# Hybrid gated block: the last block's projected tiles and first x tiles, and the list's price for the sums' loads

## The chip, the cores and the metric

The kernel runs on one core of one Trainium2 chip. The metric is the device time of one execution in microseconds. Before the change it is 2861.07 us, the median of three runs (2854.05 to 2863.21).

## What is computed

A layer of a streaming encoder, on x of 2048 tokens by 1024 features in float32. Only the end of the mixer and what follows it matters here:

```python
y = sigmoid(ga) * (att @ w_att_proj) + sigmoid(gm) * (mlstm_out @ w_mlstm_proj)
x = x + y @ w_out
hn = rms_norm(x, ffn_norm_g)
x = x + square(relu(hn @ w_up)) @ w_down
return rms_norm(x, final_norm_g)
```

`att` is a banded attention over chunks of 64, `mlstm_out` a recurrent matrix memory, and both read projections of the normed x.

## The kernel before

**Tiles and products.** The tokens are cut into four blocks of 512 (b = 0 to 3), the features into eight tiles of 128 (j = 0 to 7); a working tile is 128 x 512, 256 KB. Each float32 product is made of three fp32r products of 512 columns, from a high part (ScalarE, lines 427 and 971) and a rest (VectorE, lines 429, 976, 978) of each operand. Blocks are taken in pairs, 0 with 1 and 2 with 3, and the large products of a pair are done by a scheme with 7 instead of 8 sub-products (`quad`, line 571 in the trace). For it, sums of operand tiles and of weight tiles are needed. Per quad, seven operand sets A[0] to A[6] are used in order; A[0] and A[1] are the tiles k and 4 + k of the first block of the pair, and A[2] to A[6] need the second block as well. One quad is 7 x 24 = 168 products.

**Weights' sums.** `sum_w` makes the weights' sums of a quad once and keeps them in memory: per half, four loads of 256 KB into four `ctx` buffers (line 391), four subtractions on VectorE (line 396), four stores. They run beside other stages, from the second projection of block 0 to the first up quads, and stand last in rank.

**The last blocks.** After the down product of blocks 0 and 1, `project(2)` and `project(3)` multiply the mixers' outputs with their projections, tile pairs in the order 0, 2, 1, 3, which gives the tiles j in the order 0, 1, 4, 5, 2, 3, 6, 7. `load_gates` brings gate tiles into `temp` buffers (line 789), `merge` multiplies gate and bank (line 797), adds the two branches (line 805) and stores the result to `ypd[b]` (line 2101). `take_y_low` loads block 2's tiles for A[0] and A[1] (line 1731). Once `project(3)` is through, `take_y_rest(k)` for k = 0 to 3 takes five `ctx` buffers, loads two tiles of each block (line 1743), makes four sums (line 1749) and splits five operands. Then come the two output quads of blocks 2 and 3. `after_out` loads the x tiles to which they are added (`load`, line 2049, eight tiles one after another) and adds them (line 2062); the new x goes to memory and into the operands of the up quads that follow.

**Buffers.** There are 16 `ctx` buffers, 6 `temp` buffers, 28 operand buffers (`rpool`) and 8 PSUM banks. All users of `ctx` share the 16.

**Order.** The program is written out by a list planner (`Flow`): each step is a generator that yields the engine that it needs, its cost in ns and, for a load, the time to its landing, as in `yield "sp", 900, 2000`; steps carry a rank, and waits and buffers delay them. The planner's order is the program's order. From it the framework makes the queue of each engine, and it may pull an instruction ahead of earlier ones when its data and its buffers are free; the program's order is then the priority. On the chip each queue is worked through in order. All DMAs are issued from SyncE's queue.

Of the kernel before, what the change touches and what calls it, by code (L numbers as in the profile page):

```python
# [45 lines left out]
N_G, N_O, N_F = 2, 2, 8  # L46
# [47 lines left out]
class Flow:  # L94
# [8 lines left out]
               dve=dict(pe=220.0, act=130.0, dve=130.0, pool=155.0), pool=dict(pe=290.0, act=130.0, dve=60.0),  # L103
               sp=dict())
# [110 lines left out]
def dve_ns(n):  # L215
    return 70 + 1.042 * n
# [7 lines left out]
class Layer:  # L224
# [156 lines left out]
    def sum_w(self, q):  # L381

        fl, V = self.fl, self.nc.vector
        for h in range(2):
            got = yield "get", self.ctx, 4
            a, b, c, d = (x[:, :512] for x in got)
            wf, td = (t[:, :, h * 512:h * 512 + 512] for t in (self.io["wf"][q], self.td[q].ap()))
            kept = [Event() for _ in range(4)]
            for n, x in ((0, a), (1, c), (3, d), (2, b)):
                yield "sp", 900, 2000  # L390
                self.nc.sync.dma_start(x, wf[n])
            for n, dst, x, y in ((0, a, c, a), (2, c, d, c), (1, a, d, a), (3, b, b, a)):
                if n == 1:
                    yield "wait", [kept[0]]
                yield "dve", dve_ns(512)
                V.tensor_sub(dst, x, y)  # L396
                fl.spawn(self.store(td[n], dst, kept[n]), 1)
            yield "wait", kept
            fl.put(self.ctx, *got)
            fl.set(self.td_ev[q][h])  # L400
# [228 lines left out]
    def dense(self):  # L629
        fl = self.fl  # L630
# [51 lines left out]
        self.banks.want = 0  # L682
        O, X, U = self.operands(), self.operands(), self.operands()
        for i in range(N_G):
# [12 lines left out]
        for i, name in enumerate(IN_ORDER):  # L697
# [3 lines left out]
            if last:  # L701
                for k in range(4):
                    fl.spawn(self.take_x2(0, k, *U), 2)
            if i == 1:
# [4 lines left out]
                yield from self.quad(*X, self.after_in(name), release=last)  # L709
        for s in range(NS):  # L710
            if s == 1:
                U = self.operands()
                for i in range(N_O):
                    if i == N_O - 1:
                        for k in range(2):
                            fl.spawn(self.take_x2(1, k, *U), 2)
                    yield from self.quad(*O, self.after_out(1, i, U), release=i == N_O - 1)
            for i in range(N_F):
                if s == 0 and len(IN_ORDER) + i in EARLY_SUMS:
                    fl.spawn(self.sum_w(EARLY_SUMS[len(IN_ORDER) + i]), 3)  # L720
                if i == 2:
                    for h in range(2):
                        fl.spawn(self.norm_mid(s, h), 3)
                if i == N_F - 2:
                    D = {}, {(m, c): [Event() for _ in range(4)] for m in ORDER for c in range(4)}
                    ring = Pool([])
                    fl.spawn(self.take_u(s, ring, *D), 0)
                if s == 0 and i == N_F - 2:
                    fl.spawn(self.gates_far(2), 3)
                if s == 0 and i == N_F - 1:  # L730
                    for b in (2, 3):
                        fl.spawn(self.recurrence_far(b), 1)
                        fl.spawn(self.attention_far(b), 1)
                yield from self.quad(*U, self.after_up(s, i), release=i == N_F - 1)
            fl.spawn(self.final(s), 2 if s else -1)
            self.banks.want = 4
            for p, m in enumerate(ORDER):
                if p == 1:
                    fl.spawn(self.residual(s), 2)
                if s == 0 and p == len(ORDER) - 1:  # L740
                    O = self.operands()
                    for b in (2, 3):
                        fl.spawn(self.take_mix(b), 1)
                yield from self.down(s, m, ring, *D)
            self.banks.want = 0
            for b in (2, 3) if s == 0 else ():
                yield from self.project(b)
                for k in range(4):
                    fl.spawn((self.take_y_low if b == 2 else self.take_y_rest)(k, *O), 2)

    def take_mix(self, b):

# [4 lines left out]
            B["mix"][i] = r  # L757
            fl.spawn(self.take_u1(self.mixd[b].ap()[i], r, B["mix_ev"][i]), 1)

    def project(self, b):  # L760

        fl, B = self.fl, self.blk[b]
        gates = {}
        go = [Event() for _ in range(5)]
        fl.spawn(self.load_gates(b, gates, go), 1)
        for n, j in enumerate((0, 2, 1, 3)):
            att = {}
            fl.set(go[n + 1])
            for x in range(2):
                some = slice(4 * x, 4 * x + 4)  # L770
                bks = yield from self.pair_tile(B["mix"][some], B["mix_ev"][some], "get")
                for n in range(2):
                    fl.spawn(self.merge(b, x, 2 * j + n, bks[n], gates, att.setdefault(n, [None, Event()])), 1)
        fl.put(self.rpool, *B["mix"])
# [17 lines left out]
    def merge(self, b, x, j, bk, gates, att):  # L792
        fl, V = self.fl, self.nc.vector
        yield "wait", [gates[x, j][1]]
        g = gates[x, j][0]
        yield "dve", dve_ns(574)
        V.scalar_tensor_tensor(g[:, :512], g[:, :512], 1.0, bk, op0=ALU.add, op1=ALU.mult)
        fl.put(self.banks, bk)
        if x == 0:
            att[0] = g  # L800
            fl.set(att[1])
            return
        yield "wait", [att[1]]
        yield "dve", dve_ns(512)
        V.tensor_add(g[:, :512], g[:, :512], att[0][:, :512])
        fl.put(self.temp, att[0])
        fl.spawn(self.store(self.ypd[b].ap()[j], g[:, :512], self.yp_ev[b][j], self.temp, g), 1)
# [927 lines left out]
    def take_y_rest(self, k, A, aev):  # L1735

        fl, V = self.fl, self.nc.vector
        got = yield "get", self.ctx, 5
        a11, a12, a21, a22, s1 = (x[:, :512] for x in got)
        for b, j, a in ((2, k, a11), (2, 4 + k, a12), (3, k, a21), (3, 4 + k, a22)):  # L1740
            yield "wait", [self.yp_ev[b][j]]
            yield "sp", 900, 2000
            self.nc.sync.dma_start(a, self.ypd[b].ap()[j])
        done = []
        for m, dst, x, y in ((2, s1, a21, a22), (5, a21, a11, a21), (3, a11, s1, a11), (4, a12, a12, a11),
                             (6, a22, None, None)):
            if x is not None:
                yield "dve", dve_ns(512)
                (V.tensor_add if m == 2 else V.tensor_sub)(dst, x, y)
            fl.spawn(self.take_split(dst, m, k, A, aev, 0.5), 1)  # L1750
            done.append(aev[m][k])
        yield "wait", done
        fl.put(self.ctx, *got)
# [274 lines left out]
        fl.put(self.ctx, z)  # L2028
        fl.spawn(self.store(self.mfar[b].ap()[g], d5, self.m_ev[b, g], self.ctx, dst), 1)

    def after_out(self, s, q, U):

        fl, nc = self.fl, self.nc
        V = nc.vector
# [5 lines left out]
        hev = [{w: Event() for w in where} for _ in range(2)]  # L2040

        def load():
            for w in ("a11", "a22", "a12", "a21"):
                for n in range(2):
                    hi, h = where[w]
                    (x,) = yield "get", self.ctx, 1
                    xt[n][w] = x
                    yield "sp", 900, 2000
                    nc.sync.dma_start(x[:, :512], self.io["xt"][2 * s + h, 4 * hi + 2 * q + n])
                    fl.set(ev[n][w])  # L2050

        fl.spawn(load(), 1)
        for n in range(2 if s > 0 and q > 0 else 0):
            fl.spawn(self.spread(ht[n], hev[n], 2 * q + n, U), 1)
# [318 lines left out]
    def build(self):  # L2373
        fl, nc = self.fl, self.nc
# [15 lines left out]
        self.fin = [f32d(f"fin{h}", 4, P, T) for h in range(2)]  # L2390
        self.ud = f32d("u", 4, 7, 4, P, T)
        self.wi = 0
        self.wtile = {}
        self.wev, self.wgot = collections.defaultdict(Event), collections.defaultdict(Event)
        self.td_ev = {q: E(2) for q in (*range(N_G, N_G + N_O + N_USUM), *range(N_Q - N_F, N_Q + 2))}
# [111 lines left out]
```

## Time and profile before

| what | value |
|---|---|
| median of three runs | 2861.07 us (2854.05 to 2863.21) |
| the profiled execution | 2857.33 us |
| its span, first to last instruction | 2855.5 us |
| granted TensorE clock | 0.997 |
| VectorE busy | 2027.8 us (71%) |
| ScalarE busy | 1550.2 us (54%) |
| DMA read and written | 433.27 and 180.36 MB |

The page gives busy times of each engine and the chain of work that ended last. PE is TensorE, PEld its weight load, DVE is VectorE, ACT ScalarE, POOL GpSimd, SP SyncE; L571 is line 571 of the kernel. Times of rows in time are us from the start of the span. Since products overlap in the array, the busy time of PE is not the time that they need; the spacing of their starts is.

### The profile page before, as it was taken

To read this page: it belongs to the slowest core of one execution; us is meant where nothing else is said; L and a number is where in the kernel's file an instruction comes from. 1 tells how busy PE (TensorE), PEld (TensorE's weight loads), DVE (VectorE), ACT (ScalarE), POOL (GpSimd) and SP (SyncE) were. 2 spreads that over 40 slices of the span, in tenths; PEclk is the share of its full clock that TensorE was granted. 3 is DMA by queue.
4 is the path that set the end of the run, shared out by engine and by line. 5 is a ranking of instruction groups with operands and counts; after the bars stand their busy time and mean duration, and the time that the engine had idled before them with its cause. 6 is when DMAs were issued, how large, how long until landed. Compare 5 with 4: busy or idle time off the path is not lost.

```text
span 2855.5 us, 39050 instructions
## 1 busy us (share of the span) xinstructions
PE 2807.1 (98%) x13576; PEld 2342.3 (82%) x13576; DVE 2027.8 (71%) x3765; ACT 1550.2 (54%) x2679; POOL 47.8 (2%) x108
## 2 busy tenths in 40 slices
PE   8999999999999999999999999999999999999998
PEld 7888888888878888878888888887887788888887
DVE  6886479868896867876666788789668644455565
ACT  4664366755444545665555665566535655555444
POOL 0000000000000000000000000000000000000000
PEclk9999999999999999999999999999999999999999
DMA  6327732367765768587888967776697655566563
GB/s 218 99 90 256 243 113 88 126 194 248 253 220 191 240 225 290 172 274 273 299 277 285 280 213 234 209 241 222 218 309 245 202 199 195 197 236 213 188 223 134
DMA packets 283174, 616.24 MB, mean 216 GB/s; under 512 B 31712, under 2 KB 48224, under 8 KB 282976
## 3 DMA queue, kind: packets, MB, share of 16 engines
q1 hardware_dynamic: 282976, 613.75, 64.9%
q8 instruction: 106, 1.74, 0.2%
q14 instruction: 92, 0.75, 0.1%
HBM read 433.27 MB, written 180.36 MB: 215 GB/s over the span
## 4 chain that ended last, share of the span: by engine, by line
PE 82%; DVE 7%; DMA 5%; ACT 3%; issue 2%; POOL 0%; SPq 0%; POOLq 0%; DVEq 0%; ACTq 0%
PE bank L571 35%; PE bank L488 12%; PE bank L489 12%; PE bank L490 12%; PE bank L599 2%; PE bank L1228 2%; PE bank L1268 2%; DMA r<-u 2%; PE bank L1299 2%; DVE wsp L429 1%; DMA ctx<-in_wf 1%; DVE r L976 1%; DMA wsum<-ctx 1%; ACT wsp L427 1%; DMA sc<-x 0%
## 5 line engine op out<-in xcount | busy, mean ns | idle before, releaser
L571 PE MATMUL bank<-r,wsp 128*128 128x512 f32 x5208 | 1193.5, 390 | 15.1 <-DVE ctx L1819 8.4
L571 PEld LDWEIGHTS bank<-r,wsp 128*128 128x128 f32 x5208 | 977.2, 188 | 225.8 <-DVE ctx L1819 8.6
L429 DVE TENSOR_TENSOR wsp<-wraw,wsp 128x1024 fp32r<-128x1024 f32 x461 | 563.3, 1222 | 346.6 <-ACT wsp L427 330.5
L427 ACT CAST wsp<-wraw 128x1024 fp32r<-128x1024 f32 x461 | 484.1, 1050 | 493.3 <-PE bank L571 189.0
L488 PE MATMUL bank<-r,wsp 128*128 128x512 f32 x1600 | 640.5, 400 | 2.4 <-DVE r L1304 1.0
L490 PE MATMUL bank<-r,wsp 128*128 128x512 f32 x1600 | 624.9, 391 | 0.0
L489 PE MATMUL bank<-r,wsp 128*128 128x512 f32 x1600 | 624.7, 390 | 0.0
L490 PEld LDWEIGHTS bank<-r,wsp 128*128 128x128 f32 x1600 | 300.4, 188 | 64.8
L488 PEld LDWEIGHTS bank<-r,wsp 128*128 128x128 f32 x1600 | 301.1, 188 | 55.1 <-DVE r L1304 1.7
L489 PEld LDWEIGHTS bank<-r,wsp 128*128 128x128 f32 x1600 | 301.4, 188 | 51.2
L971 ACT CAST r<-r 128x512 fp32r<-128x512 f32 x240 | 146.2, 622 | 88.1 <-DMA r<-u 75.4
L976 DVE TENSOR_TENSOR r<-r 128x512 fp32r<-128x512 f32 x240 | 161.1, 688 | 41.6 <-ACT r L971 40.2
L1819 DVE TENSOR_TENSOR ctx<-bank,ctx 128x512 f32<-128x512 f32 x174 | 119.0, 687 | 82.5 <-PE bank L571 80.9
L1283 ACT ACTIVATE sc<-sc,scs 128x640 f32<-128x640 f32 (+4 forms) x128 | 97.4, 761 | 74.5 <-DVE scs L1280 71.9
L1811 ACT COPY ctx<-bank 128x512 f32<-128x512 f32 x174 | 100.9, 581 | 67.6 <-PE bank L571 62.1
L396 DVE TENSOR_TENSOR ctx<-ctx,ctx 128x512 f32<-128x512 f32 x112 | 76.7, 689 | 75.7 <-DMA ctx<-in_wf 60.2
L2178 ACT ACTIVATE ctx<-ctx 128x512 f32<-128x512 f32 x96 | 60.6, 632 | 110.5 <-DVE ctx L1819 110.4
L1274 DVE CUSTOM_DVE_ANT_0 sc<-bank,bias 128x320 f32<-128x320 f32 (+3 forms) x240 | 105.1, 461 | 16.7 <-PE bank L1268 13.9
L1228 PE MATMUL bank<-r,r 128*128 128x256 f32 (+1 forms) x672 | 107.8, 281 | 1.9 <-DVE r L1304 1.6
L1228 PEld LDWEIGHTS bank<-r,r 128*128 128x128 f32 x672 | 98.1, 189 | 12.8 <-DVE r L1304 4.6
L1304 DVE TENSOR_TENSOR r<-bank,r 128x512 fp32r<-128x512 f32 (+1 forms) x168 | 96.4, 594 | 6.5 <-ACT r L1302 5.5
L1268 PE MATMUL bank<-r,r 128*128 128x320 f32 (+3 forms) x480 | 88.1, 309 | 1.8 <-DVE ctx L1652 0.9
(290 smaller groups left out, 2837.7 us busy)
## 6 DMA issues: line engine op xcount, KB each, us to landing
wraw<-in_wf SPq DMA_DIRECT2D x170, 512.0 KB, 4.4
wraw<-wsum SPq DMA_DIRECT2D x136, 512.0 KB, 3.9
r<-u SPq DMA_DIRECT2D x224, 256.0 KB, 4.1
wraw<-in_w SPq DMA_DIRECT2D x104, 512.0 KB, 3.9
u<-ctx SPq DMA_DIRECT2D x128, 256.0 KB, 2.6
ctx<-in_wf SPq DMA_DIRECT2D x112, 256.0 KB, 4.4
wsum<-ctx SPq DMA_DIRECT2D x112, 256.0 KB, 3.9
u<-tmp SPq DMA_DIRECT2D x96, 256.0 KB, 3.3
```

Of the source, the lines that this page charges most:

```text
L427: nc.scalar.copy(w[:, 0], raw)
L429: nc.vector.tensor_sub(w[:, 1], raw, w[:, 0].bitcast(F32))
L488: mm(ps, lh, rh, start=first, stop=False)
L489: mm(ps, lh, rl, start=False, stop=False)
L490: mm(ps, ll, rh, start=False, stop=last)
L571: mm(ps, wv[:, x, k, n], a[:, y], start=new and k == 0 and x == y == 0, stop=k == 3 and x == 1, skip_group_check=True)
L971: self.nc.scalar.copy(dst[:, 0], src)
L976: self.nc.vector.tensor_sub(dst[:, 1], src, dst[:, 0].bitcast(F32))
L1228: nc.tensor.matmul(bk[:, c0:c0 + w], st, sl[:, x, o:o + w], start=n == 0, stop=n == total - 1)
L1268: nc.tensor.matmul(bks[x][:, :w], q[:, y, i * P:(i + 1) * P], kf[:, f * P + x * w:f * P + x * w + w], start=y == 0, stop=y == 1)
L1274: nc.vector.tensor_tensor_reduce(out=e[:, x * w:x * w + w], in0=bks[x][:, :w], in1=br[:, j0 + x * w:j0 + x * w + w], op0=ALU.add, op1=ALU. ...
L1819: nc.vector.tensor_add(t[:, o:o + 512], ps, t[:, o:o + 512])
```

## The change

Three things are edited. The result of `merge` for block 3 goes to a `ctx` buffer and stays there (`self.y3`), without store and load; `take_y_rest` uses these tiles as a21 and a22, and takes three `ctx` buffers of its own, one k at a time as the tiles appear. `take_y_rest` is spawned ahead of `project(3)`, with rank 1 instead of 2, and so is the first output quad's `after_out`, whose loads of x wait for an event that `project(3)` sets at its half. In the list, a load of `sum_w` takes 5000 ns to its landing, where it took 2000, and a load of `take_y_rest` 3000.

```diff
@@ sum_w
-                yield "sp", 900, 2000
+                yield "sp", 900, 5000
                 self.nc.sync.dma_start(x, wf[n])
@@ dense
             if s == 1:
-                U = self.operands()
...
-                    yield from self.quad(*O, self.after_out(1, i, U), release=i == N_O - 1)
+                    yield from self.quad(*O, self.after_out(1, i, U) if i > 0 else first_out, release=i == N_O - 1)
...
-            for b in (2, 3) if s == 0 else ():
-                yield from self.project(b)
+            if s == 0:
+                yield from self.project(2)
                 for k in range(4):
-                    fl.spawn((self.take_y_low if b == 2 else self.take_y_rest)(k, *O), 2)
+                    fl.spawn(self.take_y_low(k, *O), 2)
+                U = self.operands()
+                go = Event()
+                first_out = self.after_out(1, 0, U, go)
+                for k in range(4):
+                    fl.spawn(self.take_y_rest(k, *O), 1)
+                yield from self.project(3, go)
@@ project
+            if n == 2 and half is not None:
+                fl.set(half)
@@ merge
         yield "wait", [att[1]]
+        if b == 3:
+            (y,) = yield "get", self.ctx, 1
+            yield "dve", dve_ns(512)
+            V.tensor_add(y[:, :512], g[:, :512], att[0][:, :512])
+            fl.put(self.temp, att[0], g)
+            self.y3[j] = y
+            fl.set(self.yp_ev[3][j])
+            return
@@ take_y_rest
-        got = yield "get", self.ctx, 5
-        a11, a12, a21, a22, s1 = (x[:, :512] for x in got)
-        for b, j, a in ((2, k, a11), (2, 4 + k, a12), (3, k, a21), (3, 4 + k, a22)):
-            yield "wait", [self.yp_ev[b][j]]
-            yield "sp", 900, 2000
-            self.nc.sync.dma_start(a, self.ypd[b].ap()[j])
+        yield "wait", [self.yp_ev[3][k]]
+        got = yield "get", self.ctx, 3
+        a11, a12, s1 = (x[:, :512] for x in got)
+        for j, a in ((k, a11), (4 + k, a12)):
+            yield "sp", 900, 3000
+            self.nc.sync.dma_start(a, self.ypd[2].ap()[j])
+        yield "wait", [self.yp_ev[3][4 + k]]
+        got += [self.y3[k], self.y3[4 + k]]
+        a21, a22 = (x[:, :512] for x in got[3:])
@@ after_out, load
+            if go is not None:
+                yield "wait", [go]
```

More of the change, by code (lines that the diff above doesn't have):

```diff
@@ L758, in take_mix, with project @@
             fl.spawn(self.take_u1(self.mixd[b].ap()[i], r, B["mix_ev"][i]), 1)
-    def project(self, b):
+    def project(self, b, half=None):
         fl, B = self.fl, self.blk[b]
@@ L2029, in conv_far, with after_out @@
         fl.spawn(self.store(self.mfar[b].ap()[g], d5, self.m_ev[b, g], self.ctx, dst), 1)
-    def after_out(self, s, q, U):
+    def after_out(self, s, q, U, go=None):
         fl, nc = self.fl, self.nc
@@ L2392, in build @@
         self.wi = 0
+        self.y3 = {}
         self.wtile = {}
```

## The prediction

> **What bounds the kernel now.** I read the page first, then the chain of waits, then the busy time by stage.
>
> ```profile
> PE 2807.1 (98%) x13576; PEld 2342.3 (82%) x13576; DVE 2027.8 (71%) x3765; ACT 1550.2 (54%) x2679; POOL 47.8 (2%) x108
> ...
> PE 82%; DVE 7%; DMA 5%; ACT 3%; issue 2%; POOL 0%; SPq 0%; POOLq 0%; DVEq 0%; ACTq 0%
> ...
> 643.48 115.90 PE bank L571 x510
> ...
> 2358.51 169.49 PE bank L571 x747
> ```
>
> TensorE is busy 98% of the span, but its records overlap, so that says little. The two long unbroken stretches of the chain do: 169.49 / 747 = 0.227 us for each product of 512 columns, and 115.90 / 510 gives the same. I call this the full rate. A stage in which (number of products x 0.227) equals its length can't be shortened by anything on another engine; where it falls short, the difference is what the change can win. Windows over the stages that the change touches (columns: window, length, busy time and count of PE, PEld, DVE, ACT, POOL, granted clock, DMA share, GB/s):
>
> ```profile
> 990.00:1000.00 10.00, 8.54 (x39) 6.78 (x38) 7.82 (x9) 3.30 (x4) 0.00 (x0) 1.00 0.97 322
> 1105.00:1115.00 10.00, 8.70 (x39) 6.93 (x38) 7.39 (x10) 3.32 (x4) 0.00 (x0) 1.00 0.97 317
> 1260.00:1275.00 15.00, 11.09 (x48) 8.51 (x47) 8.04 (x11) 8.01 (x13) 0.00 (x0) 1.00 0.86 278
> 1300.00:1310.00 10.00, 8.46 (x38) 6.70 (x37) 6.02 (x8) 4.26 (x7) 0.00 (x0) 1.00 0.82 267
> ...
> 2086.00:2130.00 44.00, 44.00 (x195) 36.42 (x194) 29.73 (x39) 10.74 (x12) 0.00 (x0) 1.00 0.95 325
> 2130.00:2140.00 10.00, 10.00 (x46) 8.28 (x45) 8.57 (x14) 5.88 (x9) 0.00 (x0) 1.00 0.79 281
> 2140.00:2150.00 10.00, 6.67 (x26) 4.25 (x24) 8.86 (x14) 4.70 (x8) 0.00 (x0) 1.00 0.86 268
> 2150.00:2162.00 12.00, 8.63 (x25) 5.21 (x26) 11.66 (x20) 6.26 (x10) 0.00 (x0) 0.86 0.79 254
> 2162.00:2249.00 87.00, 86.93 (x384) 71.67 (x383) 71.40 (x101) 55.22 (x86) 0.00 (x0) 1.00 0.69 224
> 2249.00:2258.00 9.00, 7.14 (x25) 5.41 (x24) 5.13 (x7) 7.06 (x11) 0.00 (x0) 0.81 0.61 207
> 2258.00:2530.00 272.00, 272.00 (x1209) 225.45 (x1208) 132.75 (x164) 148.40 (x214) 0.00 (x0) 1.00 0.60 202
> ```
>
> The last block's projection (2086 to 2130, 195 products) runs at full rate: 195 x 0.227 = 44.3 of 44 us. So do 2162 to 2249 (87.2 of 87) and 2258 to 2530. The start of the output quads does not: from 2130 to 2162 stand 46 + 26 + 25 = 97 products, 22.0 us of work in 32 us, **10.0 us lost**. At 2249 to 2258, 25 products leave 3.3 us lost. In the four short windows of the weights' sums 1.1 + 1.1 + 4.1 + 1.4 = **7.8 us** are lost. So the change's three places hold 21.1 us together, 0.74% of the run.
>
> What TensorE waits for from 2130 to 2162, and what VectorE does there (its groups, then single rows in time):
>
> ```profile
> PE bank L571 <- DVE ctx L2062: 3.4, 2, 1.7
> PE bank L571 <- ACT r L973: 2.8, 4, 1.3
> ...
> L978 DVE SCALAR_TENSOR_TENSOR r<-ctx,r 128x512 fp32r<-128x512 f32 x19 | 12.9, 685 | 0.3 <-ACT r L973 0.2
> L1749 DVE TENSOR_TENSOR ctx<-ctx,ctx 128x512 f32<-128x512 f32 x16 | 10.8, 684 | 3.0 <-DMA ctx<-yp 3.0
> ...
> 2131.43 0.69 DVE L1749 TENSOR_TENSOR ctx<-ctx,ctx 128x512 f32<-128x512 f32 x1 [3.03 <-DMA ctx<-yp]
> ...
> 2149.90 0.69 DVE L2062 TENSOR_TENSOR ctx<-bank,ctx 128x512 f32<-128x512 f32 x1 [1.14 <-DMA ctx<-in_xt]
> ```
>
> The bound there is VectorE, busy 8.57 + 8.86 + 11.66 = 29.1 of 32 us: all 16 sums (L1749) and 19 of the 20 splits (L978) of the operands from `take_y_rest` fall into this stretch, and the first starts at 2131.43, after TensorE has left the projection. Its two idle times, 3.0 and 1.1 us, are the loads that the change removes or moves.
>
> **The change part by part.**
>
> *Straight into the operands.* Before, a tile of block 3 is added (L805), stored, and loaded again:
>
> ```profile
> 2136.29 0.38 SPq L2101 DMA_DIRECT2D yp<-tmp  x1
> ...
> 2143.25 0.38 SPq L1743 DMA_DIRECT2D ctx<-yp  x1
> ...
> yp<-tmp SPq DMA_DIRECT2D x16, 256.0 KB, 4.2
> ...
> ctx<-yp SPq DMA_DIRECT2D x24, 256.0 KB, 4.1
> ```
>
> From the issue of the last store to the landing of the last load that is 2143.25 - 2136.29 + 4.1 = 11.1 us, gone for 8 tiles: 8 stores and 8 loads of 256 KB, some 16 x 0.38 = 6.1 us of SyncE's queue. VectorE's work stays: the addition writes a `ctx` tile instead, at the same 512 elements. But it can start earlier. The projection makes the tiles in the order 0, 1, 4, 5, 2, 3, 6, 7, so k = 0 and 1 have both their tiles at half of it, and their 8 sums and 10 splits may run beside the second half. The room there:
>
> ```profile
> 2112.00:2130.00 18.00, 11.52 (x15) 1.00 1.00 352
> ...
> 2153.51 0.68 DVE L1749 TENSOR_TENSOR ctx<-ctx,ctx 128x512 f32<-128x512 f32 x1
> 2154.12 0.69 DVE L978 SCALAR_TENSOR_TENSOR r<-ctx,r 128x512 fp32r<-128x512 f32 x1
> ...
> L797 DVE SCALAR_TENSOR_TENSOR tmp<-tmp,bank 128x512 f32<-128x512 f32 x19 | 12.8, 684 | 10.9 <-DMA tmp<-gate 8.3 <-PE bank L490 2.6
> ```
>
> 18 - 11.52 = 6.5 us idle, which at 0.6 us a piece (2153.51 to 2154.12, start to start) takes some 10 of the 18. So VectorE wins 10 x 0.6 + 3.0 + 1.1 = 10.1 us against the stretch after 2130, as much as TensorE loses there. Bounds: at least the two waits, 4.1 us; at most the whole 10.0. I take **8.5**, near the upper end, because the queue's 29.1 of 32 us is the row that sets it, and leave one wait of the sort of ACT's (1.3 us) to remain.
>
> The row 2150 to 2162 also has a granted clock of 0.86: ten products take 4.09 us, 0.41 each, right behind a gap of 1.71 us.
>
> ```profile
> 2150.65 4.09 PE L571 MATMUL bank<-r,wsp 128*128 128x512 f32 x10 [1.71 <-DVE ctx L2062]
> ```
>
> The Trainium skill ("TensorE: Matmul & The Clock Gate", "What's actually happening") puts the fall to half rate behind an idle window of about 3.4 us. This trace shows half rate behind a shorter gap, in a stretch that was thinly filled before; going by the rule, a remaining gap costs only itself, and going by the row it costs another 10 x 0.18 = 1.8 us, and the gain would be 6.7 instead of 8.5.
>
> *First x tiles during the projection.* 8 loads of 256 KB (2.1 MB, 6 us at 352 GB/s) move ahead into 2108 to 2130, where the DMA share is 1.00; the 8 stores and most of the reloads leave the same stretch, so it is no fuller. Their wait (1.1 us) is counted above. The wait on `go` holds no engine, only the list's thread. Queued behind them on SyncE are gate loads; VectorE already waits 8.3 us for those from 2086 to 2130 and TensorE loses nothing, since 8 banks lie between. Cost 0; if that cover were gone, up to 8.3.
>
> *Ctx buffers.* 8 tiles of block 3, 3 for each of four k and 8 x tiles ask for 28 of 16 buffers. k = 0 and 1 give back 10 before the last are needed. I take 0; below it nothing, above it one wait for a k to finish: 9 VectorE steps, 9 x 0.69 = 6.2 us.
>
> *At 2249 to 2258.* The window before it has VectorE at 71.40 of 87 us, and all of it also after the change. I take 0 of the 3.3, bounds 3.3 won or lost.
>
> *Sums' loads.* 112 loads get 3 us more in the list, so that their subtractions stand later behind them.
>
> ```profile
> DVE ctx L396 <- DMA ctx<-in_wf: 60.2, 31, 5.7
> ...
> ctx<-in_wf SPq DMA_DIRECT2D x112, 256.0 KB, 4.4
> ...
> L1743 SPq DMA_DIRECT2D ctx<-yp x16: 319/352/1557, 2060.0 to 2143.2; - x16
> ...
> L789 SPq DMA_DIRECT2D tmp<-gate x32: 319/414/722, 1997.0 to 2122.2; - x32
> ...
> L396 DVE TENSOR_TENSOR ctx<-ctx,ctx x112: 679/691/695, 240.5 to 1482.6; 128x512 f32<-128x512 f32 x112
> ```
>
> VectorE stands 60.2 us at L396, and 7.8 of them reach TensorE. A load really takes 4.4 us against 2.0 in the list, so 5.0 would remove most of the waits, if the queues kept the list's order. They don't: an L1743 load, which the list issues after the projection, is out at 2060.0, before gate loads of that projection (to 2122.2). Steps are pulled forward as soon as their buffers are free, and a subtraction pulled forward waits as before. Bounds: 7.8 won; 7.8 lost, if the reshuffle doubles the waits. I take **1.5** won.
>
> **Sum:** 8.5 + 0 + 0 + 0 + 1.5 = 10.0 us. The profiled execution took 2857.3 us (span 2855.5 and 1.8 around it): 2847.3. The median of the runs is 3.7 higher, 2861.1, which would give 2851.1; I say **2848**. About 0.3%, 8.6 us, is what can be told from no change.
>
> **Rivals.**
> 1. *The wait only changes its name.* VectorE is the bound after 2130, and if the early sums don't find their place (the queue's order is fixed, and gate waits of 8.3 us stand in it), only 4.1 us go, and the sums' reshuffle gives or takes as much. For it: 35 of 36 steps stand after 2130 now. Against it: the data of k = 0 and 1 are there from half of the projection on, near 2110. Time 2857.3 - 4.1 = 2853.
> 2. *Slower: the sums hold the buffers.* With 3 us more on each of four loads in a row, a sum holds 4 of 16 `ctx` for 12 us more in each of 28 halves, 336 us in all between 240 and 1483. The copies out of PSUM (L1811) take from the same pool; once two sums overlap (8 buffers) and a quad's own 8 tiles are out, the next copy waits, its bank isn't cleared and TensorE stands. It decides from about half the halves on: 14 x 1.4 us (the size of the losses at 1300) = 20, less 8.5, is 2869. For it: DMA shares of 0.97 in those windows. Against it: no wait for `ctx` reaches TensorE today, and sums come last in rank.
> 3. *All three places heal:* 10.0 + 3.3 + 7.8 = 21.1, 2836. It needs the queues to follow the list.
>
> **How the numbers follow.** The forecast has 0.48, rival 1 0.24, rival 2 0.16, rival 3 0.12. The forecast reaches past 8.6 us in most of its range: faster 0.60 (0.48 and 0.12), same 0.24, slower 0.16. The range takes in rival 3 and the milder half of rival 2: 2834 to 2865. The likeliest case's own is 2841 to 2853.
>
> **What would show it.** Right: no `yp<-tmp` stores and `ctx<-yp` loads of block 3 (8 of each fewer); L1749 starting near 2110 instead of 2131; 97 products from the end of the projection in under 24 us; in_xt loads before it ends. Wrong: the projection below full rate, or L805 waiting; L396's 60.2 us far from that; new waits of L1811.

## The result and the profile after

The changed kernel takes 2847.26 us, the median of six runs (2843.84 to 2850.95); six runs of before beside it give 2861.09 (2854.05 to 2863.21). The ratio is 0.9956, 95% interval 0.9943 to 0.9969: 13.8 us, or 0.44%, faster. The profiled execution of after took 2843.84 us (span 2842.1), against 2857.33 of before.

TensorE's own line on the page of after hardly moves, as its records overlap:

```profile
PE 2804.1 (99%) x13576; PEld 2342.9 (82%) x13576; DVE 2028.9 (71%) x3767; ACT 1549.7 (55%) x2677; POOL 48.6 (2%) x108
```

The windows by stage say more; the columns are those of the prediction, and the edges follow the shifted stages:

```profile
990.00:1000.00 10.00, 9.30 (x42) 7.40 (x41) 9.51 (x11) 3.46 (x4) 0.00 (x0) 1.00 0.90 295
1107.00:1117.00 10.00, 7.85 (x35) 6.20 (x34) 8.61 (x11) 5.47 (x7) 0.00 (x0) 1.00 0.78 237
1258.00:1273.00 15.00, 15.00 (x68) 12.18 (x67) 9.34 (x13) 8.51 (x13) 0.00 (x0) 1.00 0.97 338
1298.00:1308.00 10.00, 9.18 (x41) 7.30 (x40) 8.99 (x11) 4.32 (x7) 0.00 (x0) 1.00 0.71 223
...
2085.00:2128.00 43.00, 43.00 (x192) 35.59 (x191) 34.70 (x49) 17.73 (x24) 0.00 (x0) 1.00 0.91 306
2128.00:2138.00 10.00, 10.00 (x46) 8.29 (x45) 10.00 (x16) 2.31 (x3) 0.00 (x0) 1.00 0.69 217
2138.00:2148.00 10.00, 8.01 (x34) 5.77 (x32) 10.00 (x17) 5.72 (x10) 0.00 (x0) 1.00 0.71 231
2148.00:2160.00 12.00, 11.59 (x51) 9.28 (x51) 10.70 (x16) 6.18 (x9) 0.00 (x0) 1.00 0.68 221
2160.00:2240.00 80.00, 80.00 (x355) 66.24 (x354) 66.88 (x96) 54.71 (x85) 0.00 (x0) 1.00 0.69 227
2240.00:2249.00 9.00, 9.00 (x41) 7.47 (x40) 6.24 (x9) 6.75 (x11) 0.00 (x0) 1.00 0.70 231
```

The projection still runs at full rate: 192 x 0.227 = 43.6 of 43 us. Behind it stand 46 + 34 + 51 = 131 products in 32 us where before had 97; at 0.227 us each that is 29.7 us of work, so 2.3 us are lost instead of 10.0. The place at 2249 has closed as well (41 products in 9 us). Of the four windows of the sums, the third is full now (68 products, 15.4 of 15 us), and the second has got worse (35 in 10 us).

What TensorE still waits for from 2128 to 2160 (the waits by line), and VectorE's groups in the projection before it, 2085 to 2128:

```profile
PE bank L571 <- ACT r L988: 1.5, 1, 1.5
PE bank L571 <- DVE ctx L2082: 0.5, 1, 0.5
PE bank L571 <- DVE r L993: 0.4, 1, 0.4
```

```profile
L804 DVE SCALAR_TENSOR_TENSOR tmp<-tmp,bank 128x512 f32<-128x512 f32 x14 | 9.5, 684 | 6.7 <-DMA tmp<-gate 6.7
L1767 DVE TENSOR_TENSOR ctx<-ctx,ctx 128x512 f32<-128x512 f32 x8 | 5.5, 686 | 0.0
L993 DVE SCALAR_TENSOR_TENSOR r<-ctx,r 128x512 fp32r<-128x512 f32 x6 | 4.1, 686 | 0.0
```

Half of the 16 sums and 6 of the 20 splits have moved ahead into the projection, and VectorE's waits on `yp` and `in_xt` are gone from the list. The first sum and the first x load, single rows in time of VectorE and of SyncE's queue:

```profile
2112.77 0.69 DVE L1767 TENSOR_TENSOR ctx<-ctx,ctx 128x512 f32<-128x512 f32 x1
```

```profile
2100.52 0.38 SPq L2069 DMA_DIRECT2D ctx<-in_xt  x1
```

The DMAs of `yp` in after (count, durations of the issue, first and last start), and VectorE's longest kind of wait:

```profile
L2121 SPq DMA_DIRECT2D yp<-tmp x8: 319/324/464, 2046.5 to 2095.7; - x8
...
L1758 SPq DMA_DIRECT2D ctx<-yp x8: 319/378/485, 2057.7 to 2141.6; - x8
```

```profile
DVE ctx L396 <- DMA ctx<-in_wf: 39.8, 18, 6.5
```

Eight stores and eight loads fewer, and the sums' subtraction (L396) waits 39.8 us where it waited 60.2.

I laid the starts of the stages of the two profiled executions side by side (the first product of each). After is 1.6 us early when the first output quad starts (2128.6 against 2130.2), 9.3 early at the first up quad behind it (2208.2 against 2217.6), 13.1 early at the second up quad (2246.3 against 2259.4), and 13.0 at the end. So the output quads brought 7.7 us, the place at 2249 brought 3.8, and everything ahead of them, the weights' sums included, 1.6. Those 1.6 are not one effect. TensorE's idle time (the length of a window less PE's busy time) fell from 6.0 to 0.8 us in the up quads of the first half (1232 to 1509) and from 5.7 to 1.3 from 1750 to 1950, and rose from 0.2 to 4.2 from 1509 to 1650.

### The profile page after: what moved, and what is told of

Same layout as the page of the kernel before. It is cut to its first block, busy times and chain, and to the rows that moved or that the text cites. A ratio compares the mean times of both kernels' runs of the same rounds, so it can differ in the third digit from the quotient of the medians.

```text
span 2842.1 us, 39060 instructions
## 1 busy us (share of the span) xinstructions
PE 2804.1 (99%) x13576; PEld 2342.9 (82%) x13576; DVE 2028.9 (71%) x3767; ACT 1549.7 (55%) x2677; POOL 48.6 (2%) x108
## 4 chain that ended last, share of the span: by engine, by line
PE 80%; DVE 9%; DMA 5%; ACT 3%; issue 2%; POOL 0%; SPq 0%; POOLq 0%; DVEq 0%; ACTq 0%
PE bank L571 36%; PE bank L488 12%; PE bank L489 12%; PE bank L490 12%; PE bank L1243 2%; DVE wsp L429 2%; PE bank L1314 2%; PE bank L1283 1%; DMA wsum<-ctx 1%; DVE sc L1289 1%; ACT wsp L427 1%; DMA ctx<-in_wf 1%; DMA r<-u 1%; PE bank L599 1%; DVE r L1319 1%
## 5 line engine op out<-in xcount | busy, mean ns | idle before, releaser
L396 DVE TENSOR_TENSOR ctx<-ctx,ctx 128x512 f32<-128x512 f32 x112 | 76.3, 688 | 55.4 <-DMA ctx<-in_wf 39.8
L1317 ACT CAST r<-bank 128x512 fp32r<-128x512 f32 (+1 forms) x168 | 81.7, 518 | 25.1 <-PE bank L1314 23.1
```

## The experiments

Two theories stood against each other. **A, the parts add:** each edit works at its own place, the tiles (direct, and spawned early) at the output quads, the list price at the sums. **B, a new draw:** whatever is edited, the list planner and the framework order all queues anew, so that stages far from the edit move by several us; the gain of after is partly luck. C and D name smaller rivals in the expectations. Where an expectation speaks of the first output quad to the first up quad, that is 336 products, 76.3 us at full rate. The expectations use 32 us behind the start of the quads in the same way: 141 products fit.

All results, sorted by the list price (ns) of a sum's load. "Beside before" is the median less that of the runs of before made on the same chip at the same time, and the ratio is taken against those runs, so medians of different rows aren't to be compared directly. "Tiles" says whether block 3's tiles stay in their buffers and are asked for early. The last three columns come from one profiled execution of each kernel: the start of the output quads, the time from there to the first up quad, and VectorE's wait at L396 for loads of weights.

| kernel | price | tiles | median us | ratio, 95% interval | beside before | quads start | quads take | L396 waits |
|---|---|---|---|---|---|---|---|---|
| before | 2000 | no | 2861.07 | | | 2130.2 | 87.3 | 60.2 |
| e2_tiles_only | 2000 | yes | 2857.82 | 0.9996 [0.9983, 1.0008] | -0.1 | 2137.7 | 84.1 | 67.1 |
| e6_list_2100 | 2100 | no | 2846.92 | 0.9952 [0.9936, 0.9967] | -13.5 | 2126.9 | 88.4 | 49.8 |
| f1_list_2100_again | 2100 | no | 2847.81 | 0.9968 [0.9958, 0.9978] | -8.5 | 2121.7 | 88.5 | 52.5 |
| f2_tiles_2100 | 2100 | yes | 2841.55 | 0.9947 [0.9929, 0.9966] | -14.8 | 2120.7 | 80.7 | 48.9 |
| f3_before_3500 | 3500 | no | 2864.52 | 1.0027 [1.0015, 1.0039] | +8.2 | 2145.9 | 86.3 | 41.7 |
| e8_sums_3500 | 3500 | yes | 2856.15 | 0.9988 [0.9978, 0.9997] | -4.3 | 2136.0 | 80.2 | 43.7 |
| e1_sums_only | 5000 | no | 2857.98 | 0.9998 [0.9990, 1.0007] | 0.0 | 2131.6 | 87.9 | 43.5 |
| after | 5000 | yes | 2847.26 | 0.9956 [0.9943, 0.9969] | -13.8 | 2128.6 | 79.6 | 39.8 |
| f4_before_8000 | 8000 | no | 2870.73 | 1.0044 [1.0028, 1.0061] | +14.4 | 2136.9 | 92.7 | 46.7 |
| e7_sums_8000 | 8000 | yes | 2865.13 | 1.0020 [1.0010, 1.0031] | +4.7 | 2142.9 | 85.5 | 43.4 |
| e3_direct_late | 5000 | late | 2855.92 | 0.9996 [0.9987, 1.0006] | -2.0 | 2127.6 | 88.6 | 39.5 |
| e4_store_early | 5000 | stored | 2860.19 | 1.0005 [0.9996, 1.0013] | +2.2 | 2133.0 | 91.6 | 35.4 |
| e5_x_late | 5000 | yes | 2846.89 | 0.9950 [0.9936, 0.9965] | -13.5 | 2129.5 | 76.4 | 36.0 |

**The sums' price alone** (before, with 5000):

```diff
-                yield "sp", 900, 2000
+                yield "sp", 900, 5000
```

> The kernel before with only the price of the sums' loads at 5000. In the changed kernel the time won sits in three places: -7.7 us from the start of the first output quad of blocks 2 and 3 to the first up quad behind them, -3.8 us in that up quad, and -2.7 us net by the start of the last up quad of blocks 0 and 1 (-5.1 around the second of those up quads, +2.4 ahead of it). Theory A (the two edits work apart): this kernel shows the last of these alone, so 0 to 4 us under before, with the loss of 10 us at the last output quads and of 3.3 us in the up quad behind them unchanged. Theory B (any edit of the list reshuffles the queues, and what is won where is chance): the output quads' loss moves too, by 3 us or more, and the time is anywhere from 6 us under to 6 us over before.

The time is that of before, 0.9998 [0.9990, 1.0007]. VectorE's wait at L396 fell by 16.7 us, from 60.2 to 43.5, and bought nothing. The output quads kept their loss, 98 products in the 32 us behind their start:

```profile
2131.60:2163.60 32.00, 25.89 (x98) 18.44 (x97) 29.59 (x48) 16.89 (x26) 0.00 (x0) 0.95 0.81 265
```

But from the first to the second up quad it takes 38.1 us, like after, and not the 41.8 of before: the place at 2249 closes without the tiles. Theory A had asked for that place to stay as it was, theory B for the quads to move by 3 us or more; neither came.

**The tiles alone** (after, with 2000 again):

```diff
-                yield "sp", 900, 5000
+                yield "sp", 900, 2000
```

> The changed kernel with the price of the sums' loads back at 2000. Theory A: 11.5 us less from the last output quads to the second up quad behind them, and nothing before, so 8 to 12 us under the kernel before; VectorE waits some 60 us at the sums' loads as before. Theory B: the first up quad's 3.8 us were the sums' doing or chance, and this kernel is 4 to 8 us under before or anywhere.

The time is that of before here too, 0.9996 [0.9983, 1.0008]. The quads gained 3.2 us and the place behind them 3.7, but the quads started 7.4 us late: the stages ahead, which the edit does not name, had lost that.

```profile
2137.70:2169.70 32.00, 27.39 (x111) 21.51 (x110) 30.25 (x46) 14.57 (x21) 0.00 (x0) 0.95 0.62 203
```

So the two halves gave 0.0 and -0.1 us, and both together -13.8. Theory A in its plain form, which asked for 8 to 12 us here, falls; what each part does at its place must be told from what the new order does elsewhere.

**Direct tiles, late sums** (after, with `take_y_rest` spawned behind `project(3)`):

```diff
+                yield from self.project(3, go)
                 for k in range(4):
                     fl.spawn(self.take_y_rest(k, *O), 1)
-                yield from self.project(3, go)
```

> The changed kernel, but the sums and splits of the output operands are asked for only behind the last projection, as before; the tiles still stay in their buffers, without store and load, and the first x tiles still load early. If the removed round trip through memory is what counts: some 7 us lost less at the output quads, as in the changed kernel (2847). If the early start of VectorE's work is what counts (10 of 18 steps ahead of the projection's end): only the two waits of 3.0 and 1.1 us go, the output quads lose 5 to 6 us more than in the changed kernel, and the time is 2851 to 2854.

No gain at the quads, 88.6 us, and 2855.92 is in neither of the two ranges. The edit did not do what its name says: VectorE's groups in the projection (2084 to 2128) still hold 5 of the 16 sums and 7 of the 20 splits, 12 steps where after has 14, since the framework pulled them forward. So this run doesn't tell the early start from the missing trip. The window of the quads, what VectorE and SyncE's queue wait for there, and TensorE's rows:

```profile
L993 DVE SCALAR_TENSOR_TENSOR r<-ctx,r 128x512 fp32r<-128x512 f32 x7 | 4.7, 689 | 0.1
L1767 DVE TENSOR_TENSOR ctx<-ctx,ctx 128x512 f32<-128x512 f32 x5 | 3.4, 689 | 0.0
```

```profile
2127.60:2159.60 32.00, 24.30 (x90) 17.16 (x89) 21.14 (x32) 12.29 (x19) 0.00 (x0) 0.89 0.43 135
```

```profile
L1758 SPq DMA_DIRECT2D ctx<-yp x8: 319/352/424, 2105.6 to 2151.7; - x8
```

```profile
DVE ctx L1767 <- DMA ctx<-yp: 5.1, 1, 5.1
DVE ctx L814 <- DMA x<-ctx: 3.0, 1, 3.0
```

```profile
SPq L1758 <- DVE r L993: 6.8, 2, 6.0
```

```profile
2127.62 15.29 PE L571 MATMUL bank<-r,wsp 128*128 128x512 f32 x66
2149.73 6.41 PE L571 MATMUL bank<-r,wsp 128*128 128x512 f32 x14 [6.81 <-ACT r L988]
```

A sum also needs block 2's tiles, and VectorE waits 5.1 us for one of them; their loads are out only by 2151.7, where after has them out by 2141.6. The rows name `ctx` buffers as what holds them up: of the last loads one stands 6.0 us in SyncE's queue until a split (L993) is done with a buffer, and the addition that makes a tile of block 3 (L814) waits 3.0 us until a new x tile has been stored from one. So a wait for block 2's tiles and for buffers has taken the place of the trip, and one gap of 6.8 us that of several short ones. That the place in the list is what gave the buffers away in this order fits, but was not tried by itself.

**Stored and loaded, but spawned early** (after, with block 3's tiles stored and loaded as before):

```diff
-        if b == 3:
-            (y,) = yield "get", self.ctx, 1
...
-        for j, a in ((k, a11), (4 + k, a12)):
+        for b, j, a in ((2, k, a11), (2, 4 + k, a12), (3, k, a21), (3, 4 + k, a22)):
+            yield "wait", [self.yp_ev[b][j]]
```

> The changed kernel, but block 3's tiles are stored and loaded again as before; the sums and splits are still asked for ahead of the last projection and the first x tiles still load early. If the early start counts: k = 0 and 1 still run beside the projection's second half, only the last tiles' round trip (11.1 us from the issue of the last store to the landing of the last load) comes late, and the time is within 3 us of the changed kernel. If the round trip counts: the output quads lose some 7 us as before, 2853 to 2856.

The quads take 91.6 us, worse than before, and 2860.19 lies above both ranges of the expectation. VectorE's wait there, the last store, and TensorE's longest gap:

```profile
DVE ctx L1757 <- DMA ctx<-yp: 6.4, 1, 6.4
```

```profile
2151.69 0.32 SPq L2111 DMA_DIRECT2D yp<-tmp  x1
```

```profile
2159.51 6.80 PE L571 MATMUL bank<-r,wsp 128*128 128x512 f32 x15 [8.61 <-ACT r L980]
```

The last tile is stored at 2151.69, where before stored it at 2136.29, so the trip itself begins 15 us later than before, and this run isn't a test of the trip alone. In these two lists neither edit alone has any of the gain at the quads. That both are needed is not shown by this: each was tried at one price, the first left the early start nearly as it was, and the quads of the kernels without the tiles alone run from 86.3 to 92.7 us.

**x tiles as before** (after, without the early `after_out`):

```diff
-                    yield from self.quad(*O, self.after_out(1, i, U) if i > 0 else first_out, release=i == N_O - 1)
+                    yield from self.quad(*O, self.after_out(1, i, U), release=i == N_O - 1)
...
-                yield from self.project(3, go)
+                yield from self.project(3)
```

> After, but the first x tiles load as before the change, once the output quads have begun. Theory A (direct tiles and early spawn carry the gain at the output quads, the x tiles at most their wait of 1.1 us): from the first to the second output quad and on to the first up quad still 5 to 8 us shorter than before, end 2847 to 2850. Theory B (every other list draws the queues anew, and a draw moves the stages ahead of the output quads by -3 to +7 us): the output quads as in A, the end anywhere from 2844 to 2856. Theory C (the x tiles ahead of the quads are what clears the start of the quads): no gain there, 2854 or more.

As fast as after, 0.9950 [0.9936, 0.9965]. The quads run at full rate from end to end, one unbroken row of 377 products:

```profile
2129.51 85.86 PE L571 MATMUL bank<-r,wsp 128*128 128x512 f32 x377
```

That edit is not needed, but this is no test of x tiles that come late: the framework pulled their loads forward by itself, to 2107.02, where before had its first at 2145.28 (SyncE's queue). Theory C, that the early x tiles clear the quads, is left untried by it.

```profile
2107.02 0.38 SPq L2067 DMA_DIRECT2D ctx<-in_xt  x1
```

**An edit with no meaning, twice** (before, with 2100 in place of 2000):

```diff
-                yield "sp", 900, 2000
+                yield "sp", 900, 2100
```

> Before, with 2100 ns in place of 2000 for a load of the weights' sums: an edit with no meaning of its own. Theory A: within 2 us of before, 2856 to 2860, each stage where it was. Theory B: single stages move by 1 to 7 us and the end by up to 5 either way, though nothing was meant to change.

> The kernel with 2100 ns once more, unchanged, because its median lay 13.5 us under before with nothing meant to change. If that was chance of one chip or hour: within 3 us of before. If the queues that come from 2100 are better ones in themselves (theory B): again 9 to 15 us under before, on whatever chip.

0.9952 and, on another occasion, 0.9968: a hundred ns in the planner's list are worth 8.5 to 13.5 us, against 13.8 of the whole change, though nothing was removed. That is over the 5 us that theory B allowed, and a little under its 9 the second time. The output quads are as bad as before:

```profile
2126.90:2158.90 32.00, 24.60 (x93) 18.94 (x91) 27.69 (x43) 14.90 (x23) 0.00 (x0) 0.84 0.76 247
```

```profile
2121.70:2153.70 32.00, 24.27 (x94) 18.18 (x93) 27.49 (x42) 15.33 (x24) 0.00 (x0) 0.89 0.77 243
```

The time comes from ahead of them: they start at 2126.9 and 2121.7. These are two executions of one kernel, so 5 us of that lies between executions; the medians differ by 0.9.

The traces show the new order itself. In before, 24 large products stand in an unbroken row from 1416.66; with 2100 ns eight small ones of another line come in between:

```profile
1416.66 5.60 PE L571 MATMUL bank<-r,wsp 128*128 128x512 f32 x24
```

```profile
1419.17 0.95 PE L2119 MATMUL bank<-ones,bias 128*128 128x2 f32 x8
```

From there to 2071, 2289 of TensorE's 13576 products are of another line than the product at the same place in before, and from 1107 on 451 of the 1926 issues in SyncE's queue. Between the two executions with 2100 ns no place differs, on any engine.

**The price as a dose, with and without the tiles.** Five more kernels, before and after each with 3500 and with 8000 and after with 2100, make pairs at five prices.

> After, with 3500 ns in place of 5000 for a load of the weights' sums, halfway to the 2000 of before. Theory A: 2846 to 2851. Theory B: the output quads shorter by 3 to 8 us, the rest moved by -4 to +7, the end anywhere from 2845 to 2860. Theory D (the time itself matters, by its size): halfway between the 2857.8 measured with 2000 and after's 2847, that is 2851 to 2854, and a wait of the subtractions of about 50 us, between 60 and 40.

> After, with 8000 ns in place of 5000 for a load of the weights' sums. Theory A: the output quads as in after (7 to 8 us shorter than before), the end 2845 to 2850. Theory B: the output quads shorter by 3 to 8 us, the stages ahead of them moved by -4 to +7, the end anywhere from 2845 to 2860. If a longer time truly takes waits out of the sums (theory D), the wait of the subtractions falls below the 39.8 us of after.

> After, with 2100 ns for a load of the weights' sums: the pair to the kernel above, which lacks the tiles. Theory A (the tiles' gain of 7 to 8 us adds to whatever the list price gives): 7 to 8 us under the kernel above. Theory B (each list is a new draw, and only the stretch of the output quads answers to the tiles): first output quad to first up quad in 76 to 86 us, against 87 to 89 without the tiles, but the end anywhere from 2843 to 2862, above or under the kernel above.

> Before, with 3500 ns for a load of the weights' sums: the pair to after with 3500, which ran 4.3 us under before. Theory A: 3 to 4 us over before, so that the tiles' 7 to 8 make up the rest. Theory B: the output quads take their 87 to 89 us, the end anywhere from 2846 to 2866.

> Before, with 8000 ns for a load of the weights' sums: the pair to after with 8000, which ran 4.7 us over before. Theory A: 12 us over before, some 2871. Theory B: the output quads take their 87 to 89 us, the end anywhere from 2846 to 2870.

Several ranges were missed. After with 3500 (2856.15) lies in the range of B alone. After with 8000 (2865.13) is slower than either theory allowed, its quads gained less than the 3 us of B, and its wait at L396, 43.4, is not under the 39.8 of after, as theory D asked. After with 2100 lies 6.3 us under f1, a little less than the 7 to 8 of A, with quads as B had them. Before with 3500 is 8.2 us slower, where A asked for 3 to 4. Before with 8000 came out where A put it (2871), but its quads (92.7) are longer than B had them.

Without tiles the five prices 2000, 2100, 3500, 5000, 8000 give ratios of 1, 0.9952 to 0.9968, 1.0027, 0.9998 and 1.0044: no dose, a scatter. Theory D (the price works by its size) falls too; the wait at L396 goes from 60.2 down to 41.7 at 3500 and that kernel is slower than before.

With the tiles each price is faster than without, by 0.0004, 0.0021, 0.0039, 0.0042 and 0.0024 of the time (the differences of the ratios, f2 against f1, which ran together). Their mean is 0.0026, with a 95% interval from their own scatter of 0.0007 to 0.0045: some 7.4 us, 2.0 to 12.9. The interval hangs on the choice of run: with the first occasion of 2100 in place of f1 the mean is 0.0023 and the interval reaches down to 0. The stage itself says it more firmly: over the whole quads the five pairs gain 3.2, 7.8, 6.1, 8.3 and 7.2 us, 6.5 in the mean (4.0 to 9.0 by their scatter). The windows of 32 us behind the start of the quads at 2100, 3500 and 8000, with tiles and then without at the two for which it is not shown above:

```profile
2120.70:2152.70 32.00, 29.55 (x125) 22.73 (x125) 28.40 (x42) 14.12 (x20) 0.00 (x0) 1.00 0.63 190
```

```profile
2136.00:2168.00 32.00, 29.69 (x126) 22.98 (x125) 25.25 (x37) 14.44 (x20) 0.00 (x0) 1.00 0.53 155
```

```profile
2142.90:2174.90 32.00, 27.01 (x105) 20.76 (x104) 30.49 (x47) 14.38 (x21) 0.00 (x0) 0.89 0.63 203
```

```profile
2145.90:2177.90 32.00, 27.37 (x103) 20.39 (x102) 28.71 (x45) 14.89 (x23) 0.00 (x0) 0.89 0.75 253
```

```profile
2136.90:2168.90 32.00, 22.71 (x85) 16.15 (x84) 25.71 (x40) 13.58 (x21) 0.00 (x0) 0.89 0.88 300
```

94 products become 125, 103 become 126, 85 become 105. So both theories hold a part: the tiles add their gain at their place at every price (A), and the order of the rest is drawn anew each time, from 13.5 us faster to 14.4 slower (B).

The tiles with 2100 ns have the lowest median of all, 2841.55 us, 0.9947 [0.9929, 0.9966]; from after (0.9956) that cannot be told apart. Since its price has no meaning, it is a lucky list, not a better kernel.

## Why the prediction was right, point by point

**The total was right, 2848 against 2847.26, but not all of its terms.** The terms added up to 10.0 us, and the two traces are 13.1 us apart behind the places that the change touches. That 2848 fell so close has a part of luck: it was taken between 2847.3 (the sum from the profiled execution) and 2851.1 (from the median).

- *What bounds it.* Held. The projection runs at full rate in every kernel here (43.5 us from its start to that of the quads in all 14 profiles), so nothing that was put beside it cost time.
- *Straight into the operands, 8.5 us.* Right in mechanism and nearly in size: 7.7 in the pair of profiles, 6.5 in the mean of five pairs. 14 of VectorE's steps moved ahead, where 10 were counted; a wait for ACT of 1.5 us remained, where 1.3 was left for it, and two more of 0.5 and 0.4. The sign that was named for it was narrowly missed: the first 97 products took 25.4 us from the start of the quads, not under 24, against 32.8 before. One reason behind it was incomplete: with the trip of 11.1 us gone and 12 steps ahead, e3 gains nothing, because block 2's loads and buffers are late next.
- *The half rate.* The choice between rule and row did not matter: the remaining gap of 1.50 us was followed by the full rate, so it cost only itself here, as the Trainium skill's rule ("TensorE: Matmul & The Clock Gate", "What's actually happening") has it for a gap that short. That rule isn't safe for such gaps: in before 1.71 and 1.86 us did bring the half rate, and there the measurement decides (last section).
- *First x tiles, 0 beyond their wait.* Held: VectorE waits 6.7 us for gates in the projection and TensorE loses nothing.
- *Ctx buffers, 0.* Held in after, where no loss of TensorE shows it. It isn't safe: in e3 a load stands 6.0 us for a buffer, close to the upper bound of 6.2 that the prediction gave.
- *At 2249, 0.* Wrong, 3.8 won, and not by the tiles: e1 closes it without them, and e8 has 42.5 us there with them, 0.7 more than before. It goes with the order, not with VectorE's load, by which it was judged; what closes it was not tried by itself.
- *Sums' loads, 1.5.* The net of everything ahead of the quads was 1.6, but the term was not of the kind that was taken. It was read as waits that heal. L396's wait did fall by a third, to 39.8 us, which the prediction had named as a sign of being wrong, and the price alone gave 0.0; single prices gave up to 13.5 us less and 14.4 more. Its bounds of 7.8 were too narrow, because they came from losses at the sums alone, while a new order moves losses in stages that have nothing to do with the sums, as that from 1750 to 1950 above, far behind the last sum. That part of the total was luck.
- *The sum.* Adding the parts is right for what they do at their places and wrong for a pair of runs: 0.0 and -0.1 made -13.8.
- *Rivals.* Rival 1 (2853) has the size of what happened to the quads at a price of 2000, where 3.2 of 11 us were won, but not its mechanism: 7 of the 16 sums ran beside the projection there. Of rival 2 the outcome exists (8000 is slower, with tiles and without), but its mechanism isn't shown: no wait of the PSUM copies for `ctx` appears in the list of waits of before with 8000. Rival 3 did not happen: the second window of the sums is worse than it was.

What stays open is by which stage's order a price wins or loses. In the second profile of the 2100 kernel TensorE's idle time fell from 6.0 to 3.8 us in the up quads, from 3.0 to 0.1 from 1750 to 1850 and from 2.9 to 1.0 from 1950 to the last projection, and the first up quad behind the output quads took 1.9 us less; none of these was tried by itself.

## What to carry to other kernels

When a planner orders the whole program, an edit has two effects: its own, read in the stage that it touches, and a new order everywhere else, here worth up to 14 us (0.5%) either way. Measure an edit of that size at several settings of something without meaning, with and without it, and compare the stage; one pair of runs measures mostly the draw. And when a load is taken out of an operand's path, ask for the other operand of the same instruction, and for the buffer that it is loaded into: in e3 both were late.

## What the hardware showed

Gaps of nearly the same length had different followers. In after, TensorE went on at 0.235 us a product behind 1.50 and 0.41 us:

```profile
2147.43 0.73 PE L571 MATMUL bank<-r,wsp 128*128 128x512 f32 x2 [1.50 <-ACT r L988]
2148.57 11.77 PE L571 MATMUL bank<-r,wsp 128*128 128x512 f32 x50 [0.41 <-DVE r L993]
```

In before, ten products behind 1.71 us took 4.09, but twelve behind 1.68 us took 3.00, 0.25 each:

```profile
2142.95 3.00 PE L571 MATMUL bank<-r,wsp 128*128 128x512 f32 x12 [1.68 <-DVE ctx L2062]
```

Nor does a well-filled stretch before the gap protect it: at 2249 in before, behind 87 us at full rate, a gap of 1.86 us was followed by 27 products in 7.99 us, 0.30 each. What does fit is where the gap lies. The granted clock of these traces falls to 0.50 for 3.41 us, or for a few times that (the last stretch of a trace ends with it), and within each of the 14 traces all such stretches start a whole number of times 3.413 us apart (in before 2151.32 and 2253.72, 30 times). So they lie on a grid. In windows on that grid (the gap of 1.68 us, then the two places with the half clock, each with the window behind it):

```profile
2141.08:2144.49 3.41, 1.73 (x8) 1.31 (x8) 3.41 (x6) 1.49 (x2) 0.00 (x0) 1.00 0.86 261
2144.49:2147.91 3.42, 2.92 (x13) 1.91 (x11) 3.42 (x6) 2.22 (x5) 0.00 (x0) 1.00 0.84 281
2147.91:2151.32 3.41, 1.60 (x6) 0.88 (x6) 2.27 (x5) 0.31 (x1) 0.00 (x0) 1.00 0.90 276
2151.32:2154.73 3.41, 3.41 (x9) 2.08 (x7) 3.41 (x7) 1.13 (x2) 0.00 (x0) 0.50 0.96 327
...
2250.31:2253.72 3.41, 1.55 (x8) 1.28 (x8) 2.36 (x4) 2.84 (x5) 0.00 (x0) 1.00 0.47 109
2253.72:2257.13 3.41, 3.41 (x10) 2.63 (x9) 1.22 (x1) 2.46 (x5) 0.00 (x0) 0.50 0.85 327
```

TensorE was busy 1.60 and 1.55 of 3.41 us ahead of the half clock, and 1.73 where none followed. Over the 14 traces, from 40 us to the last product, every grid window at the full clock in which TensorE was busy for less than 48% was followed by the half clock, and none with more than 52%; between the two both occur. So a gap of 1.7 us can bring the half rate or cost only itself, by how it lies in this grid. This was read from the traces and not tried by itself.
